# Output projection of a hybrid trunk: the first token tile's high and low parts in buffers of their own and made in mid-attention, the last weights' low parts on VectorE, and the skip weights in one transfer

## The chip, the cores and the metric

The kernel runs on one core of a Trainium2 chip. The metric is the device time of one execution in microseconds, as the median of several runs. The engines are named as the profile names them: PE is TensorE (PEld its weight loads), DVE is VectorE, ACT is ScalarE, POOL is GpSimd, SP is SyncE, whose queue (SPq) issues nearly all DMA transfers of this kernel.

## The reference

Two layers work on 256 context tokens and 1024 latent tokens of width 1024, all in float32. The first layer is a Mamba-2 mixer (a state-space scan in chunks of 128, forward and backward), the second is attention with 16 query heads and 4 key heads. Each layer is fed with a normalised and modulated input; the modulation comes from a matrix product of the condition vectors with `mod_w`. What matters here:

```python
sh, scl, gt = jnp.split(sc @ mod_w[i] + mod_b[i], 3, axis=-1)       # modulation, both layers
in_lat = rmsnorm(h_lat, norm_w[i]) * (1.0 + scl[:, None]) + sh[:, None]

y = (y + dsk * xs.astype(F32))                                       # layer 1: skip weights, one per head (32)

o_lat = (ol * jax.nn.silu(gl)) @ out_w                               # layer 2: gated attention, output projection
h_lat = h_lat + gt[:, None] * o_lat
return rmsnorm(h_lat, final_norm_w)
```

The attention output has 1024 tokens by 1024 columns, and the output projection multiplies it with a 1024 by 1024 weight.

## The kernel before, in words

**Products in three passes.** A float32 product is made from operands split into a high part (a rounded copy, `fp32r`, made by ACT) and a low part (the rest, made by a subtraction on DVE or POOL). `mm3` (L167 to L170) issues three matmuls for each pair: high by high, low by high, high by low. The profile shows them as lines L168, L169 and L170, in every stage that uses the helper.

**The order of the work is planned.** Each stage describes its operations to a `Plan` (L52): engine, dependencies, a rank, an estimated duration, and which ring buffers it takes and uses. `Plan.order` (L82) plays a list schedule: whenever an engine is free in its model, it starts the operation of lowest rank whose dependencies are over and whose buffers are free. The instructions are then issued in the order of the starts, and each engine works through its own list in that order on the chip. A ring gives its buffers in the order in which they were reserved by `hold`, except for the rings named in `ANY`. An operation on SP is a DMA issue; the model counts 0.38 us for the issue, and its transfers follow each other (0.9 us for a usual one, 0.05 us for one marked `small`).

**Start.** The first plan begins with the modulation of layer 1. `sums` (L283) loads `mod_w` in 32 pieces of 256 KB (L297, tile `spare`, a ring of 20 pieces) and multiplies each with the two condition vectors (L303; each float32 product shows as two matmuls). `normalised` (L332) loads the ten token tiles (L339, tile `xt`) and scales them to unit mean square. When the last piece of `mod_w` has been multiplied, its sums are turned into columns (L313, L319, L326), and `modulated` (L356) makes the layer's input, from which all products of the first layer are made. Seven small tables are loaded with the helper `small` (L280; its line is L281) at ranks -850 and up: `convw`, `convb`, `dtbias`, `a_bc`, `mnw` and, with two transfers, `dskip`, the skip weights. Head by head, `dskip[j*64:(j+1)*64]` takes 16 numbers that lie two apart in HBM, the same 16 for each of 64 partitions. `dskip` is first read at L822, in the first chunk of the scan. `mnw` is loaded from an array that lies in HBM as it lies in SBUF: 128 rows of 16 numbers.

**Attention.** The last plan (L1581 on) works through 16 units, a unit being one pair of heads by 512 query tokens: units 0 to 7 are the first 512 tokens (`at[0]`), units 8 to 15 the others (`at[1]`). For each of ten key tiles PE makes scores (L1675), ACT takes the exponential (L1680, tile `P`, a ring of six), PE multiplies with the values (L1691, tile `ot`), and DVE and POOL add the exponentials up (L1656, `acc`; POOL takes seven key tiles, DVE three). At the end of a unit the two sums are added (L1700), PE sums them over the partitions (L1713, tile `dn`, the divisors), ACT copies that (L1717), DVE takes the reciprocal (L1721), POOL multiplies with the gate (L1722), and DVE writes the unit's part of `at` (L1723). Meanwhile PE and DVE make the row maxima of a later unit (L1474, L1621). PE's order in this stage is written out by hand (`turns`).

**Output projection.** The weight comes in 16 pieces of 128 by 512 (`wr`, a ring of four, L1753). Each is split: high part by ACT (L1760), low part at L1763. The pieces of the first four weight rows (`kt` 0 to 3, tiles `woh` and `wol`) are split during attention, with POOL making the low parts. The pieces of the last four (`kt` 4 to 7, tiles `khw` and `klw`) take the place of the keys and so wait for the last scores; there DVE and POOL make the low parts in turn. `project_out(t)` (L1777) does one tile of 128 tokens: `high` (L1786, ACT) and `low` (L1790, DVE) split its 128 by 1024 slice of `at` into two buffers of the ring `P`, then PE makes 48 matmuls (`product`, 6 for each `kt`), then the result is scaled, added to the residual (`h`, L1811 and L1825), normalised and stored (L1822 to L1846). The tables that this needs (`tab`, L1772) take the place of the two `acc` buffers. Ranks: unit `u` has about 100u, tile `t`'s parts have 1600 + 100t, its products 1700 + 100t + kt. Tiles 0 to 3 read `at[0]`, which is complete when unit 7 is, tiles 4 to 7 read `at[1]`.

The parts of a tile wait for their place in the ring, behind the 160 buffers that attention itself reserves:

```python
            hh, hl, hs, x = plan.hold("P"), plan.hold("P"), plan.hold("sc"), {}
            a = plan.op("ACT", high, done, R - 100, 1.12, takes=[hh])
            a = plan.op("DVE", low, [a], R - 100, 1.15, takes=[hl], uses=[hh])
```

Of the kernel before, what the change touches and what calls it, by code (L numbers as in the profile page):

```python
# [9 lines left out]
FR = mybir.dt.float32r  # L10
# [10 lines left out]
KT = D // 128  # L21
# [9 lines left out]
WE = 4  # L31
# [106 lines left out]
def rows(ap, parts):  # L138
    return bass.AP(tensor=ap.tensor, offset=ap.offset, ap=[[0, parts]] + [list(d) for d in ap.ap])
# [6 lines left out]
def emit(tc, A, out):  # L146
    nc = tc.nc
    V, S, G, T, Q = nc.vector, nc.scalar, nc.gpsimd, nc.tensor, nc.sync
# [15 lines left out]
    m_d = scratch("m_d", [2, 4096])  # L164
# [40 lines left out]
    convw = P0.tile([128, 32, 5], FT, name="convw")  # L205
    convb = P0.tile([128, 32], FT, name="convb")
    mnw = P0.tile([128, 16], FT, name="mnw")
# [40 lines left out]
    dskip = SM.tile([128, 16], FT, name="dskip")  # L248
    dtb = SM.tile([128, 1], FT, name="dtbias")
    dtbias = dtb[64:128]  # L250
    a_bc = SM.tile([128, 64], FT, name="a_bc")
# [3 lines left out]
    for b in ub:  # L255
# [4 lines left out]
    plan = Plan({"piece": 20, "xt": 4, "raw": 4, "wraw": 2, "mraw": 2, "wparts": 4, "pj": 2, "ub": 2, "ch": NCH, "zs": 2, "tc": 2,  # L260
                 "st": 1, "yd": 1, "yo": 1, "xst": 1, "Bt": 1, "PV": 1, "xw": 3, "tm": 1, "lab": NLAB, "W0": 2, "W1": 2, "es": 3})
# [15 lines left out]
    first = [plan.op("-", change("su"), us=0.)]  # L277
# [116 lines left out]
    for b in range(3):  # L394
        modulated(b, xs[(0, 2, 6)[b]:(2, 6, 10)[b]], cols, -800 + 100 * b)

    rest = [small(-850 + i, *p) for i, p in enumerate(
        [(convw, A["conv_w"]), (convb, A["conv_b"]), (dtbias, A["dt_bias"]), (a_bc, rows(A["a_log"], 128)), (mnw, A["m_norm_w"])] +
        [(dskip[j * 64:(j + 1) * 64], bass.AP(tensor=A["m_d"].tensor, offset=A["m_d"].offset + j, ap=[[0, 64], [2, 16]]))
         for j in range(2)])]  # L400


    second = [plan.op("-", change("su2", reuse_waits="tile"), list(ready_in.values()), us=0.)]
# [493 lines left out]
    done = [None]  # L897
# [95 lines left out]
    with ExitStack() as st:  # L993
# [262 lines left out]
        a = plan.op("SP", norm_weights, [opened], HEAD, us=.76, small=True)  # L1256
# [291 lines left out]
        R = HEAD  # L1548
# [21 lines left out]
    with ExitStack() as st:  # L1570
# [7 lines left out]
            return psum("sc", [128, 2, 512])  # L1578

        NP, NU = 6, len(units)  # L1580
        plan = Plan({"q": 3, "sc": 3, "ot": 1, "dn": 1, "P": NP, "accP": 1, "accV": 1, "mx": 2, "rb": 2, "sg": 2, "ob": 2, "wr": 4})  # L1581
        qs3.append([S4.tile([128, 512], FR, name=f"q2{i}") for i in range(3)])
        at = [S4.tile([128, 8, 512], FT, name=f"at{i}") for i in range(2)]
        setup = plan.op("POOL", lambda: empty_rows(qs3[2]), [], -1000, .6)
# [1 line left out]
        def p_tile(dt=FT):  # L1586
            return S4.tile([128, 1024], dt, tag="P", bufs=NP, name="P")
# [150 lines left out]
        wparts, X4 = {}, {}  # L1738
# [6 lines left out]
        for kt in range(KT):  # L1745
            for h in range(2):
                raw, t = plan.hold("wr"), {}
                c = slice(h * 512, (h + 1) * 512)
                R = 100 * (4 + 2 * kt + h) + 50 if kt < WE else 100 * NU + 10 * kt + 5 * h

                def bring(kt=kt, c=c, t=t):
                    t["w"] = WO.tile([128, 512], FT, tag="wr", bufs=4, name="wr")
                    Q.dma_start(t["w"], A["a_out_w"][kt * 128:(kt + 1) * 128, c])  # L1753

                def part(i, kt=kt, c=c):
                    return early[i][:, kt, c] if kt < WE else late()[i][:, kt - WE, c]

                after = last_scores if kt >= WE else [finished[3 + 2 * kt + h]]
                a = plan.op("SP", bring, [], R - 80 if kt < WE else 100 * NU - 150 + kt, takes=[raw])
                a = plan.op("ACT", lambda t=t, f=part: S.activation(f(0), t["w"], AF.Copy), [a] + after, R, .63, uses=[raw])  # L1760
                odd = (2 * kt + h) % 2
                wparts[kt, h] = plan.op("POOL" if odd or kt < WE else "DVE", lambda t=t, f=part, E=G if odd or kt < WE else V:
                                        E.tensor_tensor(f(1), t["w"], f(0).bitcast(FT), op=OP.subtract), [a], R,  # L1763
                                        1.44 if odd or kt < WE else .8, uses=[raw])


        tabs = {}
# [9 lines left out]
        def project_out(t):  # L1777
            b, c = divmod(t, 4)
            R = 100 * NU + 100 + 100 * t
            hh, hl, hs, x = plan.hold("P"), plan.hold("P"), plan.hold("sc"), {}  # L1780
            src = at[b][:, :, c * 128:(c + 1) * 128]
            done = [finished[u] for u in range(NU) if units[u][0] == b]

            def high():
                x["h"] = p_tile(FR).rearrange("p (k t) -> p k t", k=KT)
                S.activation(x["h"], src, AF.Copy)  # L1786

            def low():
                x["l"] = p_tile(FR).rearrange("p (k t) -> p k t", k=KT)
                V.tensor_tensor(x["l"], src, x["h"].bitcast(FT), op=OP.subtract)  # L1790

            a = plan.op("ACT", high, done, R - 100, 1.12, takes=[hh])
            a = plan.op("DVE", low, [a], R - 100, 1.15, takes=[hl], uses=[hh])
            mm = a
            for kt in range(KT):
                def product(kt=kt):
# [63 lines left out]
def layout(inp):  # L1860
    import numpy as np
    f=lambda n: np.asarray(inp[n])
    d = {}
    d['x']=f('x')[0]; d['ctx']=f('ctx')[0]
    cols=lambda v: v.reshape(-1,128).T
    d['cc']=np.stack([cols(f('c')[0]), cols(f('c_ctx'))],-1)
    d['norm_w']=np.stack([cols(f('norm_w')[i]) for i in range(2)],1)
    d['mod_w']=f('mod_w'); d['mod_b']=f('mod_b')
    d['mod_bc']=np.stack([cols(f('mod_b')[i][:2048]) for i in range(2)],1)
    d['final_norm_w']=f('final_norm_w')  # L1870
    w=f('m_in_w')[0]
    d['w_in']=w[:,:6144].reshape(8,128,48,128).transpose(2,1,0,3).reshape(48,128,1024)
    d['w_dt']=w[:,6144:].reshape(8,128,64).transpose(1,0,2).reshape(128,512)
    d['conv_w']=f('m_conv_w')[0].reshape(5,32,128).transpose(2,1,0)
    d['conv_b']=cols(f('m_conv_b')[0])
    d['a_log']=f('m_a_log')[0].reshape(64); d['dt_bias']=f('m_dt_bias')[0].reshape(64,1)
    d['m_d']=f('m_d')[0]
    d['m_norm_w']=cols(f('m_norm_w')[0])
    d['m_out_w']=f('m_out_w')[0]
    a=f('a_in_w')[0]  # L1880
    tile4=lambda w: w.reshape(8,128,512).transpose(1,0,2).reshape(128,4096)
    d['wqkv']=np.stack([tile4(a[:,j*512:(j+1)*512]) for j in range(3)])
    d['wg']=a[:,1536:].reshape(8,128,8,128).transpose(2,1,0,3).reshape(8,128,1024)
    d['a_out_w']=f('a_out_w')[0]
    d['q_norm']=f('a_q_norm')[0]; d['k_norm']=f('a_k_norm')[0]
    r,c=np.meshgrid(np.arange(16),np.arange(64),indexing='ij')
    inv=(np.float32(10000.0)**(-np.arange(0,32,2,dtype=np.float32)/np.float32(32))).astype(np.float32)
    ar=r.reshape(-1).astype(np.float32)[:,None]*inv; ac=c.reshape(-1).astype(np.float32)[:,None]*inv

    ang=np.stack([ar,ac],1)  # L1890
    cs=np.cos(ang); sn=np.sin(ang)
    cos=np.stack([cs,cs],2).reshape(1024,64); sin=np.stack([-sn,sn],2).reshape(1024,64)
    d['rope']=np.stack([cos,sin],1).reshape(8,128,2,64).transpose(1,0,2,3)
    return {k:np.ascontiguousarray(v,dtype=np.float32) for k,v in d.items()}
# [17 lines left out]
```

## Time and profile before

| | |
|---|---|
| median of 3 runs | 1996.26 us (1993.16 to 1997.48) |
| the profiled execution: span from first to last instruction | 1992.2 us |
| what the median has beside that span | 4.06 us |
| PE busy | 1923.3 us, 97% of the span |
| DVE, ACT, POOL busy | 1450.7, 1114.1, 1199.4 us |
| mean granted clock of PE | 0.989 |
| attention | from about 1503 to 1886 us of the span |
| products of the output projection | from 1885.8 to 1983.2 us |

The profile is of one execution, and the page gives it no time of its own beside the span; a time of the run is therefore taken as the span and the 4.06 us by which the median is longer. In the profile's rows, the first two numbers are the start and the duration in microseconds; "x8" says how many instructions were merged into the row; the bracket at the end is the engine's idle time just before the row and what ended it. A tile's name before the arrow is what is written, the names after it are what is read.

### The profile page before, as it was taken

The numbers are of one execution on the slowest core, as the hardware profiler recorded it, in microseconds if no ns is written. First come the engines' busy times: TensorE is split into PE (matmuls) and PEld (weight loads), VectorE is DVE, ScalarE is ACT, GpSimd is POOL, SyncE is SP. The second block draws the span as 40 slices with busy tenths as digits, with TensorE's granted clock in tenths as the row PEclk, the third lists the DMA queues.
The fourth block names the chain that finished last, engine by engine and source line by source line (L and its number), as shares of the span: only waits on it lengthen the run. The fifth ranks groups of instructions, "written<-read, shape, count | busy, mean of one in ns | idle before, by whom it ended". The sixth has DMA issues, their size and how long they took to land.

```text
span 1992.2 us, 30263 instructions
## 1 busy us (share of the span) xinstructions
PE 1923.3 (97%) x10552; PEld 1448.4 (73%) x10552; DVE 1450.7 (73%) x1734; ACT 1114.1 (56%) x2046; POOL 1199.4 (60%) x973
## 2 busy tenths in 40 slices
PE   5799999999999999999999999999999999999998
PEld 1578888888888888888878878877775444444476
DVE  1585887887969796867545898768675888888643
ACT  2537768666667777677644775533224454444521
POOL 1212766676757585768379788764355677776722
PEclk8899999999999999999999999999999999999999
DMA  6114463635363545356586675552232011110033
GB/s 246 64 32 131 129 187 115 186 104 174 115 190 104 149 137 175 121 151 175 162 278 206 224 253 187 165 152 93 77 109 83 32 39 48 48 46 24 9 104 106
DMA packets 162125, 255.48 MB, mean 128 GB/s; under 512 B 21466, under 2 KB 57178, under 8 KB 161972
## 3 DMA queue, kind: packets, MB, share of 16 engines
q1 hardware_dynamic: 160820, 251.71, 41.1%
q8 instruction: 83, 1.36, 0.3%
q10 hardware_dynamic: 1152, 1.84, 0.3%
q14 instruction: 70, 0.57, 0.1%
HBM read 210.78 MB, written 42.63 MB: 127 GB/s over the span
## 4 chain that ended last, share of the span: by engine, by line
PE 85%; DVE 6%; DMA 2%; issue 2%; ACT 2%; POOL 2%; SPq 1%; DVEq 0%; POOLq 0%; ACTq 0%
PE pj L168 10%; PE pj L169 10%; PE pj L170 10%; PE sc L1675 7%; PE ot L1691 7%; PE ob L168 7%; PE ob L170 6%; PE ob L169 6%; PE yo L849 3%; PE st L730 3%; PE sc L1474 2%; DVE acc L657 2%; PE yd L807 2%; PE sc L168 2%; PE sc L170 2%
## 5 line engine op out<-in xcount | busy, mean ns | idle before, releaser
L168 PE MATMUL pj<-inh,whi 128*128 128x512 f32 (+1 forms) x1152 | 442.0, 384 | 5.1 <-DVE dv L465 3.2
L169 PE MATMUL pj<-inl,whi 128*128 128x512 f32 (+1 forms) x1152 | 410.1, 356 | 0.8 <-POOL inl L379 0.8
L170 PE MATMUL pj<-inh,wlo 128*128 128x512 f32 (+1 forms) x1152 | 410.4, 356 | 0.0
L168 PEld LDWEIGHTS pj<-inh,whi 128*128 128x128 f32 x1152 | 219.1, 190 | 34.4 <-DVE dv L465 3.6
L170 PEld LDWEIGHTS pj<-inh,wlo 128*128 128x128 f32 x1152 | 218.2, 189 | 32.1
L169 PEld LDWEIGHTS pj<-inl,whi 128*128 128x128 f32 x1152 | 219.3, 190 | 26.9 <-POOL inl L379 1.2
L657 DVE SCALAR_TENSOR_TENSOR acc<-ub,convw,acc 128x1282 f32<-128x1282 f32 x128 | 229.2, 1791 | 10.5 <-ACT acc L654 6.4
L766 POOL TENSOR_SCALAR_AFFINE_SELECT lab<-lab 128x512 f32<-128x512 f32 x160 | 148.6, 934 | 143.0 <-DMA lab<-la_d 117.6
L772 ACT ACTIVATE W<-lab,u_t 128x128 f32<-128x128 f32 x640 | 203.4, 391 | 51.6 <-POOL lab L766 23.0
L1656 POOL TENSOR_TENSOR acc<-acc,P 128x1024 f32<-128x1024 f32 x80 | 192.5, 2406 | 64.5 <-ACT P L1680 62.9
L1680 ACT ACTIVATE P<-sc 128x1024 f32<-128x1024 f32 x160 | 162.7, 1025 | 115.7 <-PE sc L1675 106.0
L1621 DVE TENSOR_REDUCE mx<-sc 128x2 f32<-128x1024 f32 (+1 forms) x140 | 167.4, 1214 | 38.6 <-PE sc L1474 37.6
L725 POOL TENSOR_TENSOR xw<-xst,te_t 128x256 f32<-128x256 f32 x144 | 145.9, 1026 | 27.6 <-PE st L730 17.8
L1691 PE MATMUL ot<-P,vv 128*64 128x512 f32 x640 | 154.7, 605 | 0.0
L614 POOL TENSOR_TENSOR wlo<-wraw,whi 128x512 fp32r<-128x512 f32 x48 | 70.9, 1477 | 122.8 <-ACT whi L611 119.1
L1675 PE MATMUL sc<-q,kh 64*128 64x512 f32 x640 | 135.9, 420 | 0.5 <-ACT P L1680 0.2
L785 DVE TENSOR_TENSOR W<-W 128x512 f32<-128x512 f32 x80 | 81.8, 1023 | 47.4 <-ACT W L772 42.4
L170 PE MATMUL ob<-whi,yl 128*128 128x512 f32 x288 | 113.4, 394 | 1.9 <-DVE yl L1073 1.4
L168 PE MATMUL ob<-whi,yh 128*128 128x512 f32 x288 | 113.9, 395 | 0.0
L169 PE MATMUL ob<-wlo,yh 128*128 128x512 f32 x288 | 112.9, 392 | 0.0
L1675 PEld LDWEIGHTS sc<-q,kh 64*128 64x128 f32 x640 | 60.0, 184 | 69.8 <-DVE mx L1621 29.6
L744 POOL TENSOR_TENSOR tm<-PV,dec_t 128x512 f32<-128x512 f32 x64 | 89.2, 1393 | 35.2 <-DVE PV L748 34.4
(285 smaller groups left out, 4446.1 us busy)
## 6 DMA issues: line engine op xcount, KB each, us to landing
lab<-la_d SPq DMA_DIRECT2D x160, 256.0 KB
wraw<-in_w_in SPq DMA_DIRECT2D x96, 256.0 KB
workvv<-in_m_out_w SPq DMA_DIRECT2D x94, 256.0 KB
mraw<-in_mod_w SPq DMA_DIRECT2D x64, 256.0 KB
es<-e_d SPq DMA_DIRECT2D x128, 128.0 KB
wraw<-in_wqkv SPq DMA_DIRECT2D x48, 256.0 KB
spare<-in_mod_w SPq DMA_DIRECT2D x32, 256.0 KB
q_d<-qs SPq DMA_DIRECT2D x64, 128.0 KB
```

The lines of the kernel that those rows point to most:

```text
L168: T.matmul(o, lh, rh, start=first, stop=False)
L169: T.matmul(o, lh, rl, start=False, stop=False)
L170: T.matmul(o, ll, rh, start=False, stop=last)
L657: V.scalar_tensor_tensor(t["a"], ub[i % 2][:, k:k + CW], convw[:, ct, k:k + 1], t["a"], op0=OP.mult, op1=OP.add)
L725: G.tensor_tensor(t[d], s["xst"][:, c], te_t[:, d, c, h4][:, :, None].to_broadcast([128, 4, 64]), op=OP.mult)
L766: G.affine_select(t["l", d], t["l", d], [[0, 4], [sgn, 128]], OP.is_ge, NEVER, base=0, channel_multiplier=-sgn)
L772: S.activation(t["w", d][:, h], t["l", d][:, h], AF.Exp, bias=u_t[:, d, c, 4 * g + h:4 * g + h + 1])
L1621: V.tensor_reduce(max_place(t["m"][0], i), o, AX.X, OP.max)
L1656: E.tensor_tensor(t[e], t["P", k0] if two else t[e], t["P", kt], op=OP.add)
L1675: T.matmul(o[:, h], (first_row[r] if n == 3 else (kh, kl, kh)[n][r, kv, k]), x[(0, 0, 1, 2)[n]][r], start=(n == 0), stop=(n == 3))
L1680: S.activation(t["P", kt], flat(t["s", kt]), AF.Exp)
L1691: T.matmul(t["o"][h * 64:(h + 1) * 64], vv[:, kt, kv], t["P", kt][:, h * 512:(h + 1) * 512], start=(kt == 0), stop=(kt == NT - 1))
```

## The change

Three things are changed.

1. The skip weights lie in HBM as a 128 by 16 array, already repeated over the partitions (made from the same 32 numbers when the inputs are laid out), and one transfer loads them; the transfer has the form of the one for `mnw`. One operation fewer stands in the first plan.
2. Tile 0 of the output projection has a ring of its own, `first`, of two buffers of 128 by 1024, for its high and low parts. Their rank is 1050 and no longer 1600, so they can be made once units 0 to 7 are finished. Tiles 1 to 7 keep the ring `P`, in which they now stand two places further ahead.
3. The low parts of the last four weight rows are all made on DVE; before, every second one was made on POOL.

```diff
     rest = [small(-850 + i, *p) for i, p in enumerate(
-        [(convw, A["conv_w"]), (convb, A["conv_b"]), (dtbias, A["dt_bias"]), (a_bc, rows(A["a_log"], 128)), (mnw, A["m_norm_w"])] +
-        [(dskip[j * 64:(j + 1) * 64], bass.AP(tensor=A["m_d"].tensor, offset=A["m_d"].offset + j, ap=[[0, 64], [2, 16]]))
-         for j in range(2)])]
+        [(convw, A["conv_w"]), (convb, A["conv_b"]), (dtbias, A["dt_bias"]), (a_bc, rows(A["a_log"], 128)), (mnw, A["m_norm_w"]),
+         (dskip, A["m_d"])])]
...
-        plan = Plan({"q": 3, "sc": 3, "ot": 1, "dn": 1, "P": NP, "accP": 1, "accV": 1, "mx": 2, "rb": 2, "sg": 2, "ob": 2, "wr": 4})
+        plan = Plan({"q": 3, "sc": 3, "ot": 1, "dn": 1, "P": NP, "accP": 1, "accV": 1, "mx": 2, "rb": 2, "sg": 2, "ob": 2, "wr": 4, "first": 2})
...
-                odd = (2 * kt + h) % 2
-                wparts[kt, h] = plan.op("POOL" if odd or kt < WE else "DVE", lambda t=t, f=part, E=G if odd or kt < WE else V:
+                wparts[kt, h] = plan.op("POOL" if kt < WE else "DVE", lambda t=t, f=part, E=G if kt < WE else V:
                                         E.tensor_tensor(f(1), t["w"], f(0).bitcast(FT), op=OP.subtract), [a], R,
-                                        1.44 if odd or kt < WE else .8, uses=[raw])
+                                        1.44 if kt < WE else .8, uses=[raw])
...
-            hh, hl, hs, x = plan.hold("P"), plan.hold("P"), plan.hold("sc"), {}
+            hh, hl, hs, x = plan.hold("P" if t else "first"), plan.hold("P" if t else "first"), plan.hold("sc"), {}
+
+            def parts():
+                return (p_tile(FR) if t else S4.tile([128, 1024], FR, tag="first", bufs=2, name="first")).rearrange("p (k t) -> p k t", k=KT)
...
-                x["h"] = p_tile(FR).rearrange("p (k t) -> p k t", k=KT)
+                x["h"] = parts()
...
-                x["l"] = p_tile(FR).rearrange("p (k t) -> p k t", k=KT)
+                x["l"] = parts()
...
-            a = plan.op("ACT", high, done, R - 100, 1.12, takes=[hh])
-            a = plan.op("DVE", low, [a], R - 100, 1.15, takes=[hl], uses=[hh])
+            early_on = 100 * (NU // 2 + 2) + 50 if t == 0 else R - 100
+            a = plan.op("ACT", high, done, early_on, 1.12, takes=[hh])
+            a = plan.op("DVE", low, [a], early_on, 1.15, takes=[hl], uses=[hh])
...
-    d['m_d']=f('m_d')[0]
+    d['m_d']=np.repeat(f('m_d')[0].reshape(16,2).T,64,axis=0)
```

## The prediction

> **What bounds the kernel now.** I read the page first, then PE's waits and the chain of waits, then the two stages that the change touches.
>
> ```profile
> span 1992.2 us, 30263 instructions
> PE 1923.3 (97%) x10552; PEld 1448.4 (73%) x10552; DVE 1450.7 (73%) x1734; ACT 1114.1 (56%) x2046; POOL 1199.4 (60%) x973
> ```
>
> PE is busy for 97% of the span, so a change is worth what it takes out of the other 69 us, and what it does to slow matmuls. The longest wait of all is at the start. PE there, while it sums the pieces of `mod_w`:
>
> ```profile
> 27.55 5.35 PE L303 MATMUL yd<-spare,cc 128*2 128x512 f32 x12
> 35.85 1.02 PE L303 MATMUL yd<-spare,cc 128*2 128x512 f32 x2 [0.92 <-DMA spare<-in_mod_w]
> 56.55 1.87 PE L303 MATMUL yd<-spare,cc 128*2 128x512 f32 x2 [19.67 <-DMA spare<-in_mod_w]
> 58.58 5.30 PE yd L303 x10
> ```
>
> From 36.88 to 56.55 PE waits 19.67 us for a piece (the last row is the chain's). Now SP's queue, the windows of the whole core, and the DMA queues in 36 to 52 us alone:
>
> ```profile
> 31.85 0.33 SPq L281 DMA_DIRECT2D mnw<-in_m_norm_w  x1
> 33.14 1.40 SPq L281 DMA_DIRECT2D dskip<-in_m_d  x2
> 35.14 2.81 SPq L297 DMA_DIRECT2D spare<-in_mod_w  x1
> 38.00 6.42 SPq L423 DMA_DIRECT2D wraw<-in_w_dt  x1
> ...
> 47.71 8.53 SPq L297 DMA_DIRECT2D spare<-in_mod_w  x5
> ```
> ```profile
> 30.00:32.00 2.00, 2.00 (x6) 0.34 (x5) 0.15 (x1) 1.85 (x3) 0.55 (x1) 1.00 1.04 404
> 34.00:36.00 2.00, 1.08 (x3) 0.09 (x2) 0.49 (x2) 1.38 (x3) 0.55 (x1) 1.00 0.76 226
> 46.00:48.00 2.00, 0.00 (x0) 0.00 (x0) 0.00 (x0) 0.00 (x0) 0.00 (x0) 0.50 0.05 0
> ```
> ```profile
> DMA packets 1703, 0.01 MB, mean 0 GB/s; under 512 B 1703, under 2 KB 1703, under 8 KB 1703
> q1 hardware_dynamic: 1703, 0.01, 4.7%
> ```
>
> The last three columns of a windows row are PE's clock, the DMA share and GB/s. The DMA moves 404 GB/s, and then, right after the two `dskip` transfers, nothing: 1703 packets in 16 us, together 0.01 MB, at 4.7% of 16 engines, which is 0.75 of one engine. The two transfers are 2 x 64 x 16 = 2048 numbers of four bytes, and at 1703 / 16 = 106 packets per us they last 2048 / 106 = 19.3 us, the length of PE's wait. The issues behind them, which elsewhere take 0.33 us like the one of `mnw`, stretch (2.81 and 6.42 us, and 8.53 for the last five): everything queued behind `dskip` waits for it, the last six pieces of `mod_w` among it.
>
> The second place is the hand-over from attention to the output projection:
>
> ```profile
> 1885.81 0.50 PE L168 MATMUL sc<-woh,P 128*128 128x512 f32 x1
> 1888.96 0.50 PE L170 MATMUL sc<-woh,P 128*128 128x512 f32 x1 [2.41 <-DVE P L1790]
> 1891.18 1.98 PE L1713 MATMUL dn<-acc,ones 128*64 128x512 f32 x4 [0.87 <-DVE acc L1700]
> 1893.09 0.80 PE L168 MATMUL sc<-woh,P 128*128 128x512 f32 x1
> 1896.66 0.40 PE L170 MATMUL sc<-woh,P 128*128 128x512 f32 x1
> ```
> ```profile
> 1886.00:1897.00 11.00, 7.71 (x20) 4.20 (x20) 11.00 (x8) 4.00 (x6) 4.04 (x2) 0.69 0.43 131
> 1897.00:1984.00 87.00, 86.22 (x370) 69.05 (x368) 33.27 (x53) 17.18 (x37) 27.32 (x24) 1.00 0.29 99
> ```
>
> PE waits for tile 0's low part, then for the divisors' input, and after that runs at a lower clock (mean 0.69) until 1896.66. After these eleven microseconds it is full: 370 products in the 87 us, 0.234 us each.
>
> **The skip weights.** Removed: 2048 packets of four bytes and one DMA issue. Added: 128 rows of 64 bytes, the shape and form of `mnw`, whose issue took 0.33 us and left the flow at 404 GB/s. So the hold goes. What is late next? Behind `dskip` stand eight transfers of 256 KB: six pieces of `mod_w` (x1 and x5), `w_dt` and `w_in`. At some 400 GB/s one takes 0.66 us. From where? Data of the transfers ahead flow until about 35.2 (226 GB/s in 34 to 36). The landing costs something beside the flow:
>
> ```profile
> 2.67 0.91 SPq L339 DMA_DIRECT2D xt<-in_ctx  x2
> 3.62 4.93 DMA spare<-in_mod_w
> ```
>
> The first piece, issued behind 2 x 512 KB, landed in 4.93 us; less 1 MB (2.62) and its own 0.66, that leaves 1.6. The first of the last five pieces is fourth in the flow: 35.2 + 4 x 0.66 + 1.6 = 39.4. PE needs 0.89 us a piece (5.35 / 6), more than the 0.66 of the flow, so five take 4.5 and end at 43.9. Before they ended at 58.58 + 5.30 = 63.88. Gain 20.0 us. Bounds: if PE stays at the half clock that it had after its wait (1.87 for a piece, 63.88 - 56.55 = 7.3 for all six), the end is 39.4 + 7.3 = 46.7, gain 17.2; if the flow alone decides, 35.2 + 8 x 0.66 + 1.6 + 0.9 = 43.0, or 41.5 with the five pieces ahead of the two weights, gain 22.4.
>
> Is the gain passed on? The token tiles are ready in time, and after the start PE waits for computation alone:
>
> ```profile
> 37.64 0.75 DVE L353 TENSOR_SCALAR xt<-xt,rsq 128x1024 f32<-128x1024 f32 x1 [0.44 <-POOL rsq L352]
> PE pj L168 <- DVE dv L465: 3.2, 1, 3.2
> ```
>
> The last token tile is scaled at 38.4, 5.5 us ahead of 43.9. That last row is PE's longest wait from 64 to 1000 us; it and all other groups of that view are for results of DVE, ACT and POOL, none for a DMA, so the whole chain moves forward and I count the 20.0 in full.
>
> At one place the Trainium skill would say otherwise. Its page "DMA: Bandwidth & Descriptors" (section "Why a DMA increments its semaphore by 16 and not by 1") lets a transfer use the largest number of engines up to 16 that divides the slowest dimension of both sides; for the 64 rows here that is 16, the 2048 packets would be over in about 1 us (an estimate by that page), and the hold would be somebody else's and would stay. The trace does not agree: 0.75 of one engine was busy, not 16. By that rule the start's term would be about 0; that result is rival B below.
>
> **Tile 0's parts and the hand-over.** From 1885.81 to 1896.66, 10.85 us, PE made 14 products (2 + 4 + 8) and the divisors. At full rate that is 14 x 0.234 + 0.99 (half of 1.98, since that ran at half clock) = 4.3 us, so 6.6 us are lost there: 2.41 + 0.87 of waiting, the rest the clock. DVE and POOL there:
>
> ```profile
> 1882.67 2.89 DVE L1723 TENSOR_TENSOR at<-ob,rb 128x512 f32<-128x512 f32 x1
> 1885.48 1.21 DVE L1656 TENSOR_TENSOR acc<-acc,P 128x1024 f32<-128x1024 f32 x1
> 1886.62 2.28 DVE L1790 TENSOR_TENSOR P<-at,P 128x1024 fp32r<-128x1024 f32 x1
> 1888.83 2.30 DVE L1700 TENSOR_TENSOR acc<-acc 128x1024 f32<-128x1024 f32 x1
> 1885.47 4.57 POOL L1763 TENSOR_TENSOR klw<-wr,khw 128x512 fp32r<-128x512 f32 x2 [0.46 <-ACT khw L1760]
> 1891.05 1.28 DVE L1763 TENSOR_TENSOR klw<-wr,khw 128x512 fp32r<-128x512 f32 x2
> 1721.29 1.21 DVE L1700 TENSOR_TENSOR acc<-acc 128x1024 f32<-128x1024 f32 x1
> ```
>
> With the parts made long before, PE can begin tile 0 at 1885.8 and has four `kt` of ready weights, 24 products or 5.6 us. The divisors' input no longer stands behind L1790. Its L1700 took 2.30 while POOL split weights, and 1.21 where POOL was idle (1721.29); POOL's splits are now DVE's. So: L1656 ends at 1886.7, then L1700, or first the two splits that are ready in the planner's model while the sum on POOL is not (rank 1640 against 1610), 0.65 each (1.28 for two). L1700 ends between 1887.9 and 1889.2. In the model PE puts one or two `kt` (1.4 us each) ahead of the divisors, so it comes to them at 1887.2 to 1888.7. A wait of 0 to 1.2 us is left, and I take 0.6. Gain 6.6 - 0.6 = 6.0. Bounds: 6.6, and, if the wait is 1.2 and again brings down the clock for half of the former stretch (some 3.4 us at half rate, 1.7), 3.7.
>
> Late next would be the last four weight rows. DVE's eight splits at 0.65 are 5.2 us. The first four are done by about 1890.5, PE needs them after 24 products and the divisors, at about 1892.4; the other four need their transfers:
>
> ```profile
> 1891.15 0.33 SPq L1772 DMA_DIRECT2D tab<-m_d  x1
> 1891.57 1.81 SPq L1753 DMA_DIRECT2D wr<-in_a_out_w  x4
> 1896.53 2.62 ACT L1760 ACTIVATE khw<-wr 128x512 fp32r<-128x512 f32 x4 [2.73 <-DMA wr<-in_a_out_w]
> ```
>
> These stood behind `tab`, which waited for the end of L1700 (1891.1). L1700 ends 2 to 3 us earlier, so they come 2 to 3 us earlier too, and meanwhile PE has tile 1's first four `kt`, as it had before. That tiles 1 to 3 stand two places further ahead in `P` gains nothing, PE being full there.
>
> I hold the skill's clock rule against the row here. "TensorE: Matmul & The Clock Gate" (section "What's actually happening") throttles PE after an idle window of about 3.4 us; here two pauses of 2.41 and 0.87 us were enough. By the rule the bound of 3.7 would be 5.4; the row decides.
>
> **The parts in mid-attention.** ACT's 1.05 us and DVE's 1.2 to 2.3 us (rows L1790 here and at the full speed of 1721.29) move to about 1715 to 1730, after unit 7's last step.
>
> ```profile
> 1702.00:1751.00 49.00, 48.66 (x300) 23.83 (x298) 41.71 (x33) 24.38 (x29) 34.90 (x17) 1.00 0.14 44
> 1719.88 2.10 ACT L1680 ACTIVATE P<-sc 128x1024 f32<-128x1024 f32 x2 [2.52 <-PE sc L1675]
> 1724.73 1.23 DVE L1621 TENSOR_REDUCE mx<-sc 128x2 f32<-128x1024 f32 x1 [1.10 <-PE sc L1474]
> ```
>
> Two units take 49 us; ACT is idle for 24.6 of them, DVE for 7.3, in pauses such as 2.52 and 1.10 us. That is the cover. Without it the price is 1.05 + 2.3 = 3.4 us once; I take 0.1. The two buffers and the last part of the chain (products' end at 1983.2 to 1992.2) change nothing.
>
> **Sum.** 20.0 + 6.0 - 0.1 = 25.9 us off the profiled 1992.2: 1966.3, and with the 4.06 between span and median 1970.4. Bounds: 17.2 + 3.7 - 3.4 = 17.5 off (1978.8) and 22.4 + 6.6 = 29.0 off (1967.3).
>
> **The rivals.**
>
> A. The hold goes, but the hand-over keeps its length: the late splits on DVE delay L1700 and the reciprocal, and the divisors' wait takes the place of the wait for the low part. For it: DVE is busy for all 11.00 us of that window. Against: DVE loses 2.28 us there and its contention with POOL. 20.0 - 0.1: 1976.4.
>
> B. The hold is not `dskip`'s, or the new transfer holds as long. For it: only the sum of the packets says whose they are. Against: `mnw`. Then 6.0 - 0.1: 1990.4.
>
> C. The start gains less, because PE stays slow or the first weights (`w_dt`, `w_in`) become late once the columns come 20 us earlier: 4 to 8 us given back, 1974 to 1978.
>
> D. Slower: the first plan, one SP operation shorter, comes out in another order and the scan's groups run worse. It has eight groups up to about 1000 us, and it becomes slower once a group loses 25.9 / 8 = 3.2 us; with 4 us each, 1970.4 + 32 = 2002. For it: the planner has no memory of the old order. Against: PE's longest wait in these 940 us is the 3.2 us above, once, and the shift in the model is at most the 0.38 us of one issue.
>
> **Chances.** Forecast 0.66, C 0.14, A 0.11, B 0.06, D 0.03. What can be told from no change is 0.2%, 4 us. All but D and a part of B (a quarter, where the hand-over fails as well) is faster: faster 0.95, within 0.2% 0.03, slower 0.02 to 0.03. The range takes in A and C, the bounds, and some 4 us for another order of the plans: 1962 to 1981.
>
> **What would show it.** Right: no stretch without DMA traffic after 34 us and `mod_w`'s last product at 41 to 47; PE's first product of the projection followed by the next without a wait for L1790, the clock at 1.00 there, the products' end about 26 us earlier; units of 24.5 us throughout. Wrong: a pause of many us on PE before 60, a wait at L1713 of over 1.2 us, or a unit longer than the others.

## The result, and the profile after

The changed kernel takes 1978.22 us (median of 4 runs, 1975.86 to 1979.85), the kernel before, timed with it, 1996.87 us (4 runs, 1993.16 to 1998.08). The ratio is 0.9909, with a 95% interval of 0.9895 to 0.9923: faster by 18.6 us where 25.9 were forecast. The profiled execution of the changed kernel lasted 1979.32 us. The page of the changed kernel:

```profile
span 1977.6 us, 30259 instructions
PE 1924.3 (97%) x10552; PEld 1447.9 (73%) x10552; DVE 1450.0 (73%) x1738; ACT 1114.0 (56%) x2046; POOL 1192.5 (60%) x969
DMA packets 160190, 255.48 MB, mean 129 GB/s; under 512 B 19531, under 2 KB 55243, under 8 KB 160037
```

The span is 14.6 us shorter, at the same number of matmuls. In the order of time (line numbers from L400 to L1760 are one lower than before, L1761 makes a low part of the weight, L1788 and L1792 are `high` and `low`):

**Start.** PE's timeline, then the windows of the core, then SP's queue:

```profile
34.37 1.02 PE L303 MATMUL yd<-spare,cc 128*2 128x512 f32 x2
36.22 1.02 PE L303 MATMUL yd<-spare,cc 128*2 128x512 f32 x2 [0.83 <-DMA spare<-in_mod_w]
38.33 1.02 PE L303 MATMUL yd<-spare,cc 128*2 128x512 f32 x2 [1.09 <-DMA spare<-in_mod_w]
42.11 7.24 PE L303 MATMUL yd<-spare,cc 128*2 128x512 f32 x10 [2.76 <-DMA spare<-in_mod_w]
```
```profile
36.00:38.00 2.00, 1.02 (x2) 0.09 (x2) 1.06 (x3) 1.26 (x4) 0.94 (x1) 1.00 0.82 233
38.00:40.00 2.00, 1.02 (x2) 0.09 (x2) 1.20 (x3) 0.11 (x2) 0.00 (x0) 1.00 0.79 200
42.00:44.00 2.00, 1.89 (x3) 0.34 (x4) 0.00 (x0) 0.00 (x0) 0.00 (x0) 0.50 0.97 351
```
```profile
28.23 0.33 SPq L297 DMA_DIRECT2D spare<-in_mod_w  x1
28.87 0.33 SPq L281 DMA_DIRECT2D convb<-in_conv_b  x1
30.14 0.57 SPq L281 DMA_DIRECT2D dtbias<-in_dt_bias  x1
31.43 0.33 SPq L281 DMA_DIRECT2D a_bc<-in_a_log  x1
32.09 0.33 SPq L281 DMA_DIRECT2D mnw<-in_m_norm_w  x1
33.38 0.33 SPq L281 DMA_DIRECT2D dskip<-in_m_d  x1
34.05 0.33 SPq L422 DMA_DIRECT2D wraw<-in_w_dt  x1
36.62 2.27 SPq L297 DMA_DIRECT2D spare<-in_mod_w  x5
```

The wait of 19.67 us is gone; the skip weights are issued in 0.33 us like `mnw`. In its place stand three waits of 0.83, 1.09 and 2.76 us. The flow falls to 233 and 200 GB/s in 36 to 40 us. Between 28.23 and 34.05 us SP issued five small tables and not one transfer of 256 KB. The last five pieces run at half clock (0.50), 1.45 us each, and end at 42.11 + 7.24 = 49.35 us; before it was 63.88. Gain 14.5.

**Mid-attention.** DVE, POOL and PE around the low part, and the windows of 49 us (as the 1702 to 1751 of before):

```profile
1708.17 2.31 DVE L1792 TENSOR_TENSOR first<-at,first 128x1024 fp32r<-128x1024 f32 x1
1710.40 1.21 DVE L1620 TENSOR_REDUCE mx<-sc 128x2 f32<-128x1024 f32 x1
1707.03 2.37 POOL L1655 TENSOR_TENSOR acc<-acc,P 128x1024 f32<-128x1024 f32 x1 [0.99 <-ACT P L1679]
1711.67 0.50 PE L1674 MATMUL sc<-q,kh 64*128 64x512 f32 x2 [1.02 <-DVE mx L1620]
```
```profile
1699.00:1748.00 49.00, 47.29 (x294) 23.35 (x294) 42.72 (x33) 25.00 (x29) 33.84 (x16) 1.00 0.14 44
```

The low part takes 2.31 us beside POOL's sum, the row maxima behind it come late, and PE waits 1.02 us for them. Two units now have 47.29 us of PE work in 49 us, where it was 48.66.

**Hand-over.** PE, its window and DVE:

```profile
1875.35 0.50 PE L168 MATMUL sc<-woh,first 128*128 128x512 f32 x1
1876.94 1.94 PE L1690 MATMUL ot<-P,vv 128*64 128x512 f32 x8
1880.41 1.08 PE L1712 MATMUL dn<-acc,ones 128*64 128x512 f32 x4
```
```profile
1875.00:1886.00 11.00, 11.00 (x46) 6.50 (x45) 11.00 (x10) 6.84 (x11) 1.26 (x1) 1.00 0.42 144
```
```profile
1876.74 1.21 DVE L1655 TENSOR_TENSOR acc<-acc,P 128x1024 f32<-128x1024 f32 x1
1877.88 1.28 DVE L1761 TENSOR_TENSOR klw<-wr,khw 128x512 fp32r<-128x512 f32 x2
1879.08 1.21 DVE L1699 TENSOR_TENSOR acc<-acc 128x1024 f32<-128x1024 f32 x1
```

PE waits for nothing: 11.00 busy of 11, at clock 1.00, where it was 7.71 at 0.69. The projection's first products even stand ahead of the last `ot`. The divisors come at 1880.41, after L1699, which now takes 1.21 us.

To compare executions, PE's matmuls are counted through (10552 in each kernel, in nearly the same order) and the time between fixed numbers is read from the trace. The columns are, in us: end of the last `mod_w` product; from there to the 500th matmul; the scan (500th to 5500th); mid-attention (9000th to 9300th); the hand-over (10100th to 10240th).

| | sums end | to 500th | scan | mid-attention | hand-over |
|---|---|---|---|---|---|
| before, profiled execution | 63.87 | 87.26 | 830.49 | 49.46 | 35.84 |
| after, profiled execution | 49.35 | 86.31 | 834.77 | 50.79 | 29.92 |
| gain | 14.5 | 0.9 | -4.3 | -1.3 | 5.9 |

The other stretches give -1.1 together, and the sum is the 14.6 of the two spans.

### The profile page after: what moved, and what is told of

Its sections match the earlier page's. It is cut to its first block, busy times and chain, and to the rows that moved or that the text cites. A ratio compares the mean times of both kernels' runs of the same rounds, so it can differ in the third digit from the quotient of the medians.

```text
span 1977.6 us, 30259 instructions
## 1 busy us (share of the span) xinstructions
PE 1924.3 (97%) x10552; PEld 1447.9 (73%) x10552; DVE 1450.0 (73%) x1738; ACT 1114.0 (56%) x2046; POOL 1192.5 (60%) x969
## 4 chain that ended last, share of the span: by engine, by line
PE 60%; DVE 5%; ACT 2%; issue 2%; DMA 1%; POOL 1%; SPq 0%; DVEq 0%; POOLq 0%; ACTq 0%
PE sc L1674 8%; PE ot L1690 7%; PE ob L168 6%; PE ob L170 6%; PE ob L169 6%; PE pj L168 4%; PE pj L169 4%; PE pj L170 4%; PE sc L1473 2%; PE sc L168 2%; PE sc L170 2%; PE yo L848 2%; PE sc L169 2%; PE st L729 1%; DVE acc L656 1%
## 5 line engine op out<-in xcount | busy, mean ns | idle before, releaser
L913 DVE SCALAR_TENSOR_TENSOR macc<-mraw,cc,macc 128x512 f32<-128x512 f32 x98 | 100.1, 1040 | 13.9 <-DMA mraw<-in_mod_w 13.9
```

## The experiments

### One part at a time: the skip weights

Only the transfer and the layout of what it reads are changed, in the kernel before:

```diff
-        [(dskip[j * 64:(j + 1) * 64], bass.AP(tensor=A["m_d"].tensor, offset=A["m_d"].offset + j, ap=[[0, 64], [2, 16]])) for j in range(2)]
+        [(dskip, A["m_d"])]          # 128 rows of 16, already repeated
```

> The kernel before with the skip weights in one transfer of 128 rows of 64 bytes, and nothing else of the change. Theory (the hold was the 2048 four-byte packets): the stretch without DMA traffic from 36 to 52 us is gone, the last product of mod_w ends at about 49 us as in the changed kernel (63.9 before), and the time falls by 14 to 15 us. Rival (the first plan, one SP operation shorter, costs the scan some of that: in the two traces the lead shrank from 15.5 us at 280 us to 9.6 us at 1200 us): it falls by 9 to 10 us. Rival (the hold belongs to another small transfer): no change.

Measured: 1981.98 us (6 runs) against 1995.33 (17 runs), ratio 0.993 (0.9917 to 0.9944), a gain of 13.3 us. The sums end at 48.65 us, the hand-over takes 35.98, mid-attention 49.45, as before. By the interval the gain is 11.2 to 16.6 us, which takes in the 14 to 15 expected. So this part alone is most of the gain, and it is smaller than the 20.0 of the prediction.

Then the transfers stay two, of 64 partitions each, at their old places, and only what they read is changed: rows of 64 bytes.

```diff
-        [(dskip[j * 64:(j + 1) * 64], bass.AP(tensor=A["m_d"].tensor, offset=A["m_d"].offset + j, ap=[[0, 64], [2, 16]]))
+        [(dskip[j * 64:(j + 1) * 64], A["m_d"][j * 64:(j + 1) * 64])
```

> The kernel before with the skip weights still in two transfers of 64 partitions each, but from the array that lies in HBM as it lies in SBUF, so 2 x 64 rows of 64 bytes in place of 2 x 1024 numbers of four bytes. The plan and the order on every engine are those of the kernel before. Theory (packets of four bytes are the hold, not the number of transfers): the hold is gone, within 2 us of the run with one transfer. Rival (the shorter plan costs the scan something): 4 to 6 us faster than the run with one transfer. Rival (a transfer over 64 partitions holds the queue whatever its rows): the hold of 16 us or more stays.

Measured: 1983.78 us, ratio 0.9941 (0.9926 to 0.9956), a gain of 11.5 us by medians. PE's timeline and SP's queue:

```profile
42.64 6.93 PE L303 MATMUL yd<-spare,cc 128*2 128x512 f32 x10 [3.31 <-DMA spare<-in_mod_w]
33.56 1.13 SPq L281 DMA_DIRECT2D dskip<-in_m_d  x2
```

The hold is gone with two transfers, and the order of the plan is that of the kernel before. So it was neither the number of transfers nor another plan, but the four-byte packets.

Last, half of them are put back into the changed kernel: 1024 packets of four bytes for the first 64 partitions, 64 rows of 64 bytes for the others.

```diff
-         (dskip, A["m_d"])])]
+         (dskip[0:64], bass.AP(tensor=A["m_d0"].tensor, offset=A["m_d0"].offset, ap=[[0, 64], [2, 16]])),
+         (dskip[64:128], A["m_d"][64:128])])]
```

> The changed kernel with the first 64 partitions of the skip weights loaded number by number again (1024 packets of four bytes) and the other 64 as rows of 64 bytes. Theory (the hold is the number of packets, 106 per us): a stretch without other traffic of 9 to 10 us, and mod_w's last product at about 54 to 57 us, between 49.4 (none) and 63.9 (2048). Rival (such a transfer holds the queue for a fixed time, or only the two of them together do): 49 or 63 us.

PE's timeline, a window of the core and the DMA queue from 36 to 43 us:

```profile
47.41 1.86 PE L303 MATMUL yd<-spare,cc 128*2 128x512 f32 x2 [10.14 <-DMA spare<-in_mod_w]
36.00:43.00 7.00, 1.12 (x3) 0.09 (x2) 1.59 (x3) 0.91 (x2) 1.49 (x2) 0.94 0.05 0
q1 hardware_dynamic: 722, 0.00, 4.5%
```

Half the packets hold for half the time: 10.14 us in place of 19.67, with 722 packets in 7 us (103 per us) and 0 GB/s. The sums end at 55.31 us, and the one run took 1982.94 us. The price is per packet. The Trainium skill, "DMA: Bandwidth & Descriptors" (section "Rules for kernel authors"), says that a strided last dimension is lowered to one descriptor per element; the packets here agree. The prediction set another rule of the Trainium skill's page, the one for the number of engines (section "Why a DMA increments its semaphore by 16 and not by 1"), against the row and found it refuted, with 0.75 of one engine busy. The trace says otherwise. The row's 4.7% is a mean over 16 engines, and each packet's own time is only 7 ns. In the kernel before, from 36 to 52 us, 92% of the packets are followed by another 149 to 152 ns later, and 150.5 ns hold 16.0 packets on average: sixteen sequences side by side. That is what sixteen engines with one packet in 150 ns each would leave, though the trace doesn't name a packet's engine; so the rule and the trace agree. What makes the transfer slow is the 150 ns from one packet to the next in each sequence: 2048 / 16 x 0.1505 = 19.3 us. Why a packet of 7 ns is followed only after 150 isn't shown.

### What broke the flow after the hold

In the changed kernel the small tables are to be issued behind the last piece of `mod_w`:

```diff
-            a = plan.op("SP", bring, first, -900 + i, takes=[hp])
+            a = X["bring"] = plan.op("SP", bring, first, -900 + i, takes=[hp])
...
-    rest = [small(-850 + i, *p) for i, p in enumerate(
+    rest = [small(-850 + i, *p, after=[X["bring"]]) for i, p in enumerate(
```

> The changed kernel with its six small tables loaded only after the last piece of mod_w. Theory (in the changed kernel five small tables take five of the eight places for transfers in flight while they carry next to no data, so that the flow falls to 200 to 230 GB/s from 36 to 40 us, PE pauses 2.8 us and then has the half clock for five pieces): the flow stays near 400 GB/s, mod_w's last product ends at 42 to 45 us in place of 49.4, and the time is 4 to 6 us below the changed kernel. Rival (the flow falls for another reason, the last pieces waiting for their place in the ring or the weights in between): the sums end at 48 to 50 and the time is that of the changed kernel. Rival (the tables come late for the first convolutions and step sizes): up to 5 us slower.

Measured: 1971.11 us (4 runs, 1968.63 to 1971.85), ratio 0.9877 (0.9864 to 0.9891). That is 7.1 us under the changed kernel, which was timed at another time; by the two ratios to the kernel before it is 6.4 us. Timed once more, the same kernel took 1971.84 us with the same ratio, 0.9877 (0.9859 to 0.9895):

> The kernel with the late small tables once more, beside the next two, in five rounds: it is the base that they are read against. All three have the same start. Both theories: 1969 to 1973.

Windows of the core and PE's timeline of the first of the two:

```profile
36.00:38.00 2.00, 1.05 (x4) 0.20 (x4) 0.93 (x1) 0.99 (x2) 1.56 (x2) 1.00 1.05 387
38.00:40.00 2.00, 2.00 (x6) 0.38 (x5) 1.00 (x2) 0.00 (x0) 0.66 (x1) 1.00 1.05 388
37.11 6.17 PE L303 MATMUL yd<-spare,cc 128*2 128x512 f32 x14 [0.95 <-DMA spare<-in_mod_w]
```

The flow stays at 387 GB/s, PE's longest wait is 0.95 us, the clock stays at 1.00, and the sums end at 43.27 us (45.27 in the second). The plan also moved `w_dt` to the front and a second transfer of `w_in` ahead of the last pieces, so no fewer bytes than before stand ahead of those. It is the tables that broke the flow.

How they do it can be read from the trace of the changed kernel. SP's waits between 25 and 50 us have this row (2.6 us in all, three times, 0.9 at most):

```profile
SPq L281 <- DMA xt<-in_x: 2.6, 3, 0.9
```

The tables wait for token tiles, with which they have nothing to do. The reason is in the semaphores: the program gives SP's transfers eight semaphores in turn, and here an issue starts only when the transfer eight issues before it, which has the same semaphore, has landed. `convb` starts at 28.87 us, when a piece of `mod_w` issued at 23.48 has landed (28.85); `dskip` starts at 33.38, when a token tile issued at 26.16 has landed (33.36). So at most eight transfers of SP are under way, and from 33.38 us on five of the eight are tables, which land only behind the large ones (36.38 to 37.13 us). Three places are left for data until then, and the flow thins out.

### The projection alone, and the two edits in it

The changed kernel with the old skip weights, so parts 2 and 3 alone (the edit is that of the first experiment, taken back):

> The kernel before with the two edits of the output projection (tile 0's parts in buffers of their own and early, the last low parts on DVE), and the old skip transfers. Theory: PE's 19.7 us wait at the start stays, no wait and no half clock at the hand-over (5.9 us gained between unit 15 and tile 1), and 1 us lost in mid-attention behind the low part: 4 to 5.5 us faster than before. Rival (the hand-over's gain is given back, or came from the start's shift): within 2 us of before.

Measured: 1993.92 us (11 runs, 1990.39 to 1994.72), ratio 0.9989 (0.998 to 0.9997), so 0.6 to 4.0 us faster. By the medians it is 1.4 us. That misses the 4 to 5.5 expected and lies in the rival's range, within 2 us of before. The trace has what was expected at its place: hand-over 29.92, mid-attention 50.75. But its start, with instructions in the order of before, is longer in this execution:

```profile
57.43 1.87 PE L303 MATMUL yd<-spare,cc 128*2 128x512 f32 x2 [20.01 <-DMA spare<-in_mod_w]
```

Here the sums end at 65.71 us (63.87 before), and the 500th matmul ends 3.3 us later. One execution can't tell whether the average start is later too. The mean granted clock points at where the 4.6 us of the two stretches went: the hand-over alone saves 6.8 us at half clock, which is 0.0017 of the mean clock, yet that is 0.9888 over the eleven runs, against 0.9884 over the seventeen of before. This suggests that half clock came back at other places; where in each run stays open. The difference between the kernel with the skip weights alone and the whole change, 1981.98 to 1978.22, is 3.8 us (4.2 by their ratios, since they were not timed together).

Now the two edits, on the kernel with the late tables. First the splits go back, every second one to POOL, with the early parts kept:

```diff
-                wparts[kt, h] = plan.op("POOL" if kt < WE else "DVE", ...
+                odd = (2 * kt + h) % 2
+                wparts[kt, h] = plan.op("POOL" if odd or kt < WE else "DVE", ...
```

> The kernel with the tables after mod_w, with every second of the last low parts made on POOL again, so only tile 0's own and early buffers are left of the projection's edits. Theory (the gain at the hand-over is the early parts', since PE then has tile 0 to do while the divisors' input is made): the hand-over takes 30 to 31 us, against 29.92 with both edits and 35.84 with none, and L1699 shows 2.3 us in place of 1.2 beside POOL. Rival (the splits on DVE bring half of it, by ending the contention): 32 to 34 us.

PE's timeline, then DVE's and POOL's:

```profile
1877.07 1.08 PE L1712 MATMUL dn<-acc,ones 128*64 128x512 f32 x4 [2.08 <-DVE acc L1699]
```
```profile
1871.26 2.31 DVE L1655 TENSOR_TENSOR acc<-acc,P 128x1024 f32<-128x1024 f32 x1
1873.50 2.38 DVE L1762 TENSOR_TENSOR klw<-wr,khw 128x512 fp32r<-128x512 f32 x2
1875.81 1.21 DVE L1699 TENSOR_TENSOR acc<-acc 128x1024 f32<-128x1024 f32 x1
1870.75 3.98 POOL L1762 TENSOR_TENSOR klw<-wr,khw 128x512 fp32r<-128x512 f32 x2
```

The hand-over takes 33.60 us; the rival, 32 to 34, was right and the theory, 30 to 31, not. While POOL splits (1870.75 to 1874.73), DVE's sum takes 2.31 us and its splits 1.19 each, where the same work took 1.21 and 0.64 with POOL idle; L1699 ends late, and PE waits 2.08 us and then runs at half clock. The one run took 1977.51 us. The Trainium skill, "SBUF — State Buffer" (section "Who interferes with whom"), says that a VectorE instruction with two SBUF inputs contends with a GpSimd instruction that reads SBUF; the rows agree, and give the price, which the page doesn't.

Then the other way: the parts of tile 0 go back into `P` at their old rank, and only the splits stay on DVE.

```diff
-            early_on = 100 * (NU // 2 + 2) + 50 if t == 0 else R - 100
+            early_on = R - 100      # and both buffers held in "P" again
```

> The kernel with the late small tables, with the second part of the change undone: tile 0's parts again take their places in the ring P, at their old rank, and only the splits of the last four weight rows stay on DVE alone. The hand-over took 35.84 us in the kernel before, 33.60 with the early parts alone and 29.92 with both edits. Theory (the two edits add up, since each takes its own wait off PE: the early parts 2.3 us, the splits 3.7): the hand-over takes 31.5 to 33 us, PE waits for the low part (about 1 us, since that is no longer beside POOL's splits) and not for the divisors' input, and the mid-attention stretch is back at 49.45 us. Rival (the early parts are what makes room on DVE for the splits; without them the eight splits, the low part and the sum stand one behind the other on DVE): the hand-over takes 34 to 37 us, as long as before, with PE waiting for the low part or the divisors' input over 2 us.

> The kernel with the late small tables, with the second part of the change undone and only the splits moved to DVE. In its trace the hand-over is 31.16 us (29.92 with both edits) and the mid-attention stretch 49.46 us (50.77). Theory: the early parts gain 1.24 us and cost 1.31 us, so the time is that of the base of the same call within 1 us. Rival (the single time of 1974.58 us is the kernel's, since a part made late costs more than the trace shows): 3 us or more above the base.

PE's timeline and DVE's, of the first:

```profile
1873.15 0.50 PE L170 MATMUL sc<-woh,P 128*128 128x512 f32 x1 [1.34 <-DVE P L1792]
```
```profile
1871.89 1.21 DVE L1792 TENSOR_TENSOR P<-at,P 128x1024 fp32r<-128x1024 f32 x1
1873.02 1.21 DVE L1699 TENSOR_TENSOR acc<-acc 128x1024 f32<-128x1024 f32 x1
1874.16 2.48 DVE L1761 TENSOR_TENSOR klw<-wr,khw 128x512 fp32r<-128x512 f32 x4
```

The hand-over takes 31.16 us, a little less than the theory's 31.5 to 33. With POOL quiet, the low part and the sum take 1.21 us each where they took 2.28 and 2.30; 1.34 us of waiting is left, and the clock stays up. So the splits alone bring 4.7 us of the 5.9, the early parts alone 2.2, and both together less than the sum, because the early parts save a wait that POOL's absence has nearly ended anyway. What they add to the splits, 1.2 us, they lose in mid-attention (49.46 here, 50.77 with them). The times agree with that: 1972.49 us (4 runs, ratio 0.9886, 0.9869 to 0.9904) beside 1971.84 for the kernel with the late tables, timed with it; a single run had given 1974.58. So the second part of the change has no gain of its own that these times show.

Last, the parts are kept but put into gaps: `high` waits for unit 12, `low` for DVE's sum of unit 14.

```diff
-            a = plan.op("ACT", high, done, early_on, 1.12, takes=[hh])
-            a = plan.op("DVE", low, [a], early_on, 1.15, takes=[hl], uses=[hh])
+            a = plan.op("ACT", high, done + [finished[NU - 4]] * (t == 0), early_on, 1.12, takes=[hh])
+            a = plan.op("DVE", low, [a] + [summed[NU - 2]] * (t == 0), early_on, 1.15, takes=[hl], uses=[hh])
```

> The kernel with the tables after mod_w, and tile 0's parts not in unit 8 but later: the high part once unit 12 is finished, the low part once DVE has added up unit 14's two sums, where no more maxima are made and DVE is idle for 5.7 us in the profile. Theory (in unit 8 the low part runs 2.3 us beside POOL's sum and delays a maximum, for which PE waits; cost 1.0 to 1.3 us): the 9000th to 9300th matmul take 49.45 us again in place of 50.8, the hand-over stays at 29.9 us, and the time is about 1.2 us below the run with the tables moved alone (1971.1), which 0.2% of noise may hide. Rival (the low part delays unit 15's divisors there): the hand-over is longer by 1 us or more.

> The kernel with the late small tables and tile 0's high and low part placed into gaps of ACT and DVE. In the trace it has a hand-over of 29.92 us and no loss in mid-attention (49.50 us where the base has 50.77). Theory (what stands in the trace stays to the end): 1.3 us under the base of the same call. Rival (what is gained in attention is lost in the spread of the half-clock stretches, which is larger): the medians differ by less than 0.7 us or with the other sign.

The window of mid-attention in the second:

```profile
1695.00:1744.00 49.00, 48.61 (x300) 23.93 (x298) 41.77 (x33) 24.42 (x29) 34.91 (x17) 1.00 0.14 44
```

The 300 matmuls of before are back in 49 us, and the hand-over stays at 29.92. In the times it is not settled: 1972.51 us (ratio 0.9881, 0.9865 to 0.9898) the first time, 1.4 over the 1971.11 of the kernel with the late tables, which was timed apart, and 1970.58 (0.9871, 0.9855 to 0.9886) the second, 1.3 under the 1971.84 timed with it. The trace's 1.3 us is what such medians scatter by. The kernels with the late tables that were timed at least four times, at 1970.6 to 1972.5 us, are faster than both kernels of the case.

### How far one execution differs from the next

> The kernel before once more, for a second trace of the same program. Theory (the 6 us of the lead that the changed kernel's trace loses between 280 and 1200 us are not the change's, but stretches of half clock that come and go from execution to execution, and the first profiled execution of before had few of them): the scan (PE's 500th to 5500th matmul, 830.5 us in the first trace of before, 834.8 in the changed kernel's) takes 831 to 835 us, and the hand-over (10100th to 10240th matmul, 35.84 us) 34.5 to 36 us. Rival (the change slows the scan): 830.5 us again.

The kernel before, once more: 1997.24 us, span 1995.5; its scan took 832.82 us, 2.3 more than in the first profile, and its hand-over 36.26, a little over what was expected. PE's instructions of the scan stand in the same order before and after the change.

Of the 4.3 us that the changed kernel lost in the scan, 1.4 stand between the 1250th and the 1500th matmul, where 3.4 us run at half clock. The second execution of before has the same at the same place, and ten of the fourteen profiled executions have it; so these 1.4 us are of the execution. Another 1.7 stand between the 1750th and the 2000th, with waits of 0.76 us for DVE and 0.52 for ACT. They are not in the three executions with the whole old hold, but in nine of the eleven others. The two without them have the late tables; so a short start does not force them, and whether it favours them stays open. The remaining 1.2 us are small pieces.

Behind the scan's column, at its 5697th matmul, PE waits once for ACT, in the changed kernel and then in the first profile of before:

```profile
1013.38 0.51 PE L168 MATMUL tr<-whi,yh 128*128 128x512 f32 x1 [3.35 <-ACT yh L1067]
```
```profile
1023.82 0.50 PE L168 MATMUL tr<-whi,yh 128*128 128x512 f32 x1 [2.09 <-ACT yh L1068]
```
```profile
1013.50:1017.00 3.50, 3.50 (x9) 2.43 (x10) 2.46 (x3) 2.02 (x4) 3.01 (x3) 0.53 0.98 347
```

This one wait differs by 1.3 us, and behind it, in the changed kernel, 3.4 us run at about half clock (the window, 0.53). From the 5500th to the 5750th matmul the changed kernel takes 1.3 us longer, more than the whole -1.1 of the other stretches. In the fourteen profiled executions the wait lay between 1.65 and 3.58 us, and the largest belongs to a kernel with the old start. So this too varies with the execution. The length of the wait alone doesn't bring the half clock: it followed waits of 1.65 and 1.91 us, and did not follow others of 2.09, 2.32 and 2.40.

## Why the prediction was right or wrong

**The start: the mechanism was right, the term mis-sized.** It was `dskip`'s 2048 packets; rival B is refuted by two contiguous transfers and by half the packets. The term said 20.0 and came out at 14.5, outside its bounds of 17.2 to 22.4. Two steps failed together. "The first of the last five pieces is fourth in the flow: 35.2 + 4 x 0.66 + 1.6 = 39.4" took 400 GB/s for granted; the flow was 200 to 233 behind the tables, and the piece was used at 42.11, 2.7 us later. The next step, "five take 4.5", held at full clock; after the 2.76 us wait they took 7.24, again 2.7 more. The bound with the half clock started from the same 39.4. (The other bound has a slip: 43.0 less two transfers of 0.66 is 41.7, not 41.5, and its gain 22.2; that changes nothing.) With the tables out of the way the sums ended at 43.3 to 46.9 us in seven executions, five of them by 44.7, against the 43.9 of the prediction: the sum was right for a flow that this change didn't bring about. The prediction counted the eight large transfers behind `dskip` as if they were under way one behind the other, and did not see that five tables held five of SP's eight places. Its reading of 0.75 of one busy engine was wrong, as shown with the half packets; the sum of 19.3 us was not built on it and held.

**No later wait of PE is for a DMA, so the gain is passed on: right.** PE's waits from 49 to 140 us are again for DVE, ACT and POOL alone. The stretch to the 500th matmul became 0.9 us shorter, but it lay between 84.5 and 88.7 us in the executions, so that is no gain of the change. Rival C gave about the right size, 1974 to 1978, for half the right reason: PE stayed slow, but the first weights were not late.

**The hand-over: 6.0 forecast, 5.9 measured, and the reason shared out wrongly.** No wait is left, where 0.6 was taken; by the prediction's sum that would have been 6.6. So the two numbers meet in part by luck. The half clock of the kernel before began at 1889.8 us, ahead of the pause of 0.87, so the pause of 2.41 alone was enough for it. The prediction gave the gain to the early parts, with the splits' move as the help for L1700; the runs show the splits' move at 4.7 alone and the early parts at 1.2 on top of it. Rival A, in which DVE's splits delay L1700, is refuted: two splits of 0.64 us stand ahead of L1699, and POOL's contention, which had made L1790 and L1700 2.2 us longer, ends.

**Mid-attention: 0.1 taken, 1.3 measured.** One unit became longer than the others, which was a sign of being wrong. "That is the cover" counted DVE's idle time (7.3 us in 49) and not what was queued behind the part: the row maxima, for which PE waits. The price without cover, 3.4 us, was a fair upper bound.

**From span to median.** Every run here lasts 1.7 us longer than its span (1979.32 and 1977.6; 1997.24 and 1995.5). The 4.06 us was therefore no constant: the profiled execution of before, at about 1993.9 us, was one of the short ones. The forecast of 25.9 off that span compares with 14.6; against medians it compares with 18.6. By the traces the gain lies under the prediction's lower bound of 17.5, by the medians above it; that the time fell into the stated range owes something to the margins and to that short execution. Of its signs, the end of `mod_w` at 41 to 47 us (49.35), the products' end 26 us earlier (14.6) and even units did not come true; the steady DMA traffic, the full clock and the missing waits at the hand-over did. Rival D, 32 us of slower groups in the scan, is not seen.

## What to carry to other kernels

A transfer that is tiny in bytes can be the longest of its stage: look for packets of four bytes and a DMA share of a few per cent while PE waits, and give such a table a contiguous layout. When a hold goes, look at what else stands in that queue, and how many transfers it lets under way at once: here tables with next to no data, issued among the large pieces, cost another 6 to 7 us, which moving them won. Idle time of an engine is no cover in itself; ask which queued instruction behind the new one is awaited, and which other engine slows it down.

## What the runs showed of the hardware

- Four-byte packets drained at 103 to 106 per us, in sixteen sequences with one packet of 7 ns every 150 ns, and nothing else moved meanwhile.
- DVE additions and splits of 128 x 1024 took 1.21 us, or 2.3 beside POOL's; POOL's own two splits took 3.98.
- The clock was at half after a wait of 2.08 us in the hand-over, but not after one of 1.34. Within each of the fourteen executions, the stretches at half clock begin at whole multiples of 3.413 us from each other, and most last 3.4 or 6.8 us. In the 3.41 us before each beginning PE was idle for 1.4 us or more, and, after the first 10 us, up to 1.9 us of idle time in such a window passed without one; so a pause's place among these windows counts as well as its length. The Trainium skill, "TensorE: Matmul & The Clock Gate" (section "What's actually happening"), has a free-running window of 3413 ns; the multiples agree, though here pauses shorter than a window were enough.
